# Six converted weight halves instead of five in the U pass, three raw buffers instead of five, and the split issued half a chunk sooner

## The chip, the cores and the metric

The kernel runs on one core of a Trainium2 chip. The metric is the time of one execution in microseconds, taken as the median of three runs. TensorE multiplies matrices, VectorE (DVE) and ScalarE (ACT) do elementwise work, GpSimd (POOL) issues the gathers, SyncE (SP) issues the weight loads.

## The reference, cut to what matters

One decoder layer: RMSNorm, eight differential-attention heads beside four mLSTM heads, an output projection, and then PEER, a layer of 16,384 experts of which each token takes 128. PEER dominates the time:

```python
act = jax.nn.gelu(jnp.einsum('td,tkd->tk', hb, ub), approximate=False)
return jnp.einsum('tk,tkd->td', gb * act, jnp.take(v, ib, axis=0))
```

where `ub` are the rows of the table `u` that a token's routing chose. All is float32.

## The kernel before, in words

For 352 of the 512 tokens the kernel does not gather expert rows. It multiplies the tokens by the whole table `u`, 128 chunks of 128 experts (the U pass), applies GELU, masks with a gate matrix, and multiplies by the whole table `v` (the V pass). For the other 160 tokens it gathers the chosen rows one by one: GpSimd issues an indirect DMA of 128 rows (`gather`, L834), and VectorE multiplies and adds 2048 columns of it (`run`, L861, at L846 or L859). Three row buffers `ug` rotate, so the gather after next but one waits for VectorE.

A float32 product is made of three matmuls (`mm3`, L90 to L92): weights are split into a high part `hi` and a low part `lo`, and so are the tokens. A chunk of `u` comes in two halves of 1024 columns. For each half, `load_half` (L73) loads it with an SP DMA into a buffer `raw`, ScalarE casts it to `hi` (L80), and VectorE subtracts `lo = raw - hi` (L81). A raw buffer is free again when its subtraction is done; a `hi`/`lo` buffer is free when TensorE has done its 24 matmuls of that half.

The stage that the change touches is the middle of the U pass, chunks 32 to 121 (90 of the 128), while the list `ru` is filled. There each chunk issues, in this order of the program: the split of the next chunk (`step`, L888, calls `uload(n + 1)`, L878), its own 48 matmuls, its GELU `at` on ScalarE (L902), one or two gate builds, and one or two gathered rows (`pace`, L1129). A gate build `q` is: VectorE writes one-hot masks `e` and products `eg` (`ebuild`, L1096 to L1099), ScalarE scales `ea` (L1101), TensorE multiplies them into the PSUM tile `pg` (`gbuild`, L1110, 12 matmuls), ScalarE copies `pg` to `stg` (L1118), and every eighth build one store of 2 MB from `stg` to `Gd` goes out on ScalarE's DMA queue (L1120). The 88 builds are spread over the chunks 32 to 110, so that about every tenth chunk has two. In that case TensorE multiplies both behind the same chunk, and the masks of the second are written behind the first.

TensorE, VectorE and GpSimd take their instructions in the order of the program here. ScalarE and SyncE take them in an order that the compiler's scheduler sets from its own estimates. Two PSUM tiles `pu` take the chunks in turn, two tiles `pg` the gate builds, and the masks have two buffers each.

In this stage there are five `hi`/`lo` buffers, all in the pool `wp`, and five raw buffers: three in `wp`, and two in the pool `rup`, which exists in this stage alone and takes the halves numbered 1 and 3 of every five. Buffers are 4 KB per partition each.

Of the kernel before, what the change touches and what calls it, by code (L numbers as in the profile page):

```python
# [9 lines left out]
R = mybir.dt.float32r  # L10
# [50 lines left out]
def body(tc, I, out):  # L61
    nc = tc.nc
    top = ExitStack()
    with top:
        top.enter_context(tc.manual_schedule(engines={mybir.EngineType.PE}))
        cp = top.enter_context(tc.tile_pool(name="cp", bufs=1))
        wp = top.enter_context(tc.tile_pool(name="wp", bufs=5))
        dp = top.enter_context(tc.tile_pool(name="dp", bufs=1, space=DRAM))

        def load_half(src, name, rawp=None):  # L70
            pool, n = rawp or (wp, 3)
            raw = pool.tile([128, 8, 128], F, name="raw" + name, tag="raw", bufs=n)
            nc.sync.dma_start(raw, src.rearrange("p (k c) -> p k c", k=8))  # L73
            return raw

        def split_half(src, name, raw=None, eng=nc.vector, rawp=None):
            raw = raw or load_half(src, name, rawp)
            hi = wp.tile([128, 8, 128], R, name="hi" + name, tag="whi")
            lo = wp.tile([128, 8, 128], R, name="lo" + name, tag="wlo")
            nc.scalar.copy(hi, raw)  # L80
            eng.tensor_tensor(lo, raw, hi.bitcast(F), op=OP.subtract)  # L81
            return hi, lo

        def split_tile(src, name, rawps=(None, None)):
            return [split_half(src[b], f"{name}_{b}", rawp=rawps[b]) for b in range(2)]

        def mm3(ps, w, k, xh, xl, cs):
            hi, lo = w[k // 8]
# [40 lines left out]
        def wsplit(i):  # L129
            if i < wz.shape[0] and i not in w:  # L130
                w[i] = split_tile(wz[i], f"z{i}")
# [89 lines left out]
        for k in range(KD):  # L221
            xpose(k, "m01", 0)
            if k in (2, 5):
                w[0].append(split_half(None, f"z0_{k}", raw0[k // 3], nc.gpsimd))
            if k == 6:
                sq(nc.scalar, "2", 0)
            if k == 8:
                sq(nc.vector, "2", 1)
                sq(nc.scalar, "3", 0)
            if k == 9:  # L230
                norm("2")
            if k == 10:
                sq(nc.vector, "3", 1)
                scale(nc.vector, "2", 0)
            if k == 11:
                norm("3")
                scale(nc.vector, "2", 1)
            if k == 13:
                scale(nc.vector, "3", 0)
            if k == 15:  # L240
                scale(nc.scalar, "3", 1)
            if k >= GLAG:
                gate_mm(gp[0], 0, k - GLAG)
        for k in range(KD - GLAG, KD):
            gate_mm(gp[0], 0, k)
        for k in range(KD):
            xpose(k, "23", 1)
            if k == 4:
                gate_evac(gp[0], 0)
                w[1].append(split_half(None, "z1_0", raw1))  # L250
                raw1 = load_half(wz[1, 1], "z1_1")
            if k == 12:
                w[1].append(split_half(None, "z1_1", raw1))
            if k >= GLAG:
                gate_mm(gp[1], 1, k - GLAG)
# [411 lines left out]
def rest(tc, I, out, L):  # L667
    nc = tc.nc
    wp, dp, mixT, ident, nfw = L["wp"], L["dp"], L["mixT"], L["ident"], L["nfw"]
    split_half, load_half, split_tile, mm3, rsqrt_small, big = (  # L670
        L[n] for n in ("split_half", "load_half", "split_tile", "mm3", "rsqrt_small", "big"))
# [15 lines left out]
    with tc.tile_pool(name="op", bufs=1) as op_, tc.tile_pool(name="pso", bufs=6, space=PSUM) as pso:  # L687
# [34 lines left out]
        for i, (p, pr) in enumerate(seq):  # L722
            dc, tbs = passes[p]
            if pr == 0:
# [3 lines left out]
                ps = {tb: pso.tile([128, 512], F, name="po", tag="po") for tb in tbs}  # L728
# [6 lines left out]
            hi, lo = (t.rearrange("p a b -> p (a b)") for t in ws.pop(i))  # L735
            for j in range(2):
                n = 2 * pr + j
# [6 lines left out]
            if p == 4 and pr in (2, 5):  # L744
                b = stores.pop(0)
# [44 lines left out]
    for b in range(2):  # L790
        cs = slice(1024 * b, 1024 * b + 1024)
        t = wp.tile([128, 8, 128], F, name="nfr", tag="raw", bufs=3).rearrange("p a b -> p (a b)")
        src = I["nfr"][0:1, cs]
# [82 lines left out]
    ru = []  # L876

    def uload(n):  # L878
        if n < len(sp) and n not in w:
            ps = [None, None]  # L880
            if ru:
                for b in range(2):
                    if ru[1] % 5 in (1, 3):
                        ps[b] = (ru[0], 2)
                    ru[1] += 1
            w[n] = split_tile(sp[n], f"d{n}", ps)

    def step(n, mid=None):  # L888
        uload(n + 1)
        ps = pmu.tile([128, 512], F, name="pu", tag="pu")  # L890
        nn = S if n < 16 else ND
        for k in range(KD):
            mm3(ps[:, :nn], w[n], k, h2h, h2l, slice(0, nn))
            if k == 7 and mid:
                mid()
        w.pop(n)
        return ps

    def u_chunk(c, mid=None):
        ps = step(16 + c, mid)  # L900
        at = h2p.tile([128, ND], F, name="at", tag="at", bufs=3)
        nc.scalar.activation(at, ps[:, :ND], AF.Gelu)  # L902
        nc.scalar.dma_start(Ad[c // 4, :, c % 4, :], at)

    with tc.tile_pool(name="tk", bufs=1) as tk, \
# [21 lines left out]
        def scores(h, p, qt):  # L927
            sk = tk.tile([128, 128], F, name="sk", tag="sk", bufs=2)
            nc.scalar.dma_start(sk, I["sk"][:, 2 * h + p, :])
            ps = pss.tile([128, TB, 128], F, name="pscore", tag="ps")  # L930
            for b in range(TB):
                nc.tensor.matmul(ps[:, b, :], qt[:, 128 * b:128 * b + 128], sk, start=True, stop=True)
            sc = tk.tile([128, TB, 128], F, name="scr", tag="scr", bufs=9)
            nc.scalar.copy(sc, ps)
            hd[h, p] = sc
            if p == 1:
                for b in (3, 0, 1, 2):
                    bg.append(head_tasks(h, b))
# [62 lines left out]
        def mid():  # L1001
            while pend:
                n, qt = pend.pop(0)
                scores(n // 2, n % 2, qt)
# [17 lines left out]
        for n in range(2, 16):  # L1022
            ps = step(n, mid)
            pend.append((n, qcopy(ps)))
            bgstep()
            if n % 4 == 2:
                bgstep()
# [32 lines left out]
        for src, dst in ((n1s, n1T), (n2s, n2T), (gs, None)):  # L1060
            pt = ptr.tile([128, ND], F, name="ptt", tag="ptt")
            for b in range(3):
                n = min(128, ND - 128 * b)
# [83 lines left out]
    with ExitStack() as sV:  # L1147
# [56 lines left out]
        for g in range(NG - 1):  # L1204
            n = GROUPS[g]
            free += [t0 + n + 2 * (j // 2) + 2 for j in range(n)]
            t0 += 2 * n
        for q in range(GROUPS[0], NK):
            g = max(x for x in range(NG) if g0s[x] <= q)
            m, n = q - g0s[g], GROUPS[g - 1]  # L1210
# [12 lines left out]
        for c in range(NK - UTAIL, NK):  # L1223
# [5 lines left out]
            for _ in range(-(-len(pro) // (NK - c))):  # L1229
                f, q = pro.pop(0)  # L1230
# [115 lines left out]
        for i, (g, hf, pr, c) in enumerate(vord[:last]):  # L1346
# [9 lines left out]
            if i == nlast - 8:  # L1356
                for b in range(2):
                    t = wp.tile([128, 8, 128], F, name="nlw", tag="raw", bufs=3)
                    src = I["nlw"][0:1, 1024 * b:1024 * b + 1024]
# [21 lines left out]
            else:  # L1381
                dc = hf
                if pr == 0:
                    ps = []
# [3 lines left out]
                hi, lo = vs.pop(i)  # L1388
# [6 lines left out]
                if tail:  # L1395
                    f, tb = tail.pop(0)
# [96 lines left out]
```

## Time and profile before

| what | value |
|---|---|
| median of three runs | 3291.85 us (3288.75 to 3292.93) |
| profiled execution | 3289.89 us, span 3288.1 us |
| TensorE matmul busy | 3222.9 us, 98% of the span |
| VectorE busy | 2323.8 us, 71% |
| ScalarE busy | 1315.1 us, 40% |
| GpSimd busy | 932.0 us, 28% |
| the stage with `ru` filled | about 1412 to 2205 us |

TensorE is busy nearly throughout; what a change in the preparation of weights can move is the idle time of TensorE that ends with such a piece of work. The share of VectorE is a mean over stages and is far higher in the stage of interest.

### The profile page before, as it was taken

To read this page: it belongs to the slowest core of one execution; us is meant where nothing else is said; L and a number is where in the kernel's file an instruction comes from. 1 tells how busy PE (TensorE), PEld (TensorE's weight loads), DVE (VectorE), ACT (ScalarE), POOL (GpSimd) and SP (SyncE) were. 2 spreads that over 40 slices of the span, in tenths; PEclk is the share of its full clock that TensorE was granted. 3 is DMA by queue.
4 is the path that set the end of the run, shared out by engine and by line. 5 is a ranking of instruction groups with operands and counts; after the bars stand their busy time and mean duration, and the time that the engine had idled before them with its cause. 6 is when DMAs were issued, how large, how long until landed. Compare 5 with 4: busy or idle time off the path is not lost.

```text
span 3288.1 us, 51152 instructions
## 1 busy us (share of the span) xinstructions
PE 3222.9 (98%) x20174; PEld 3038.4 (92%) x20174; DVE 2323.8 (71%) x3521; ACT 1315.1 (40%) x2219; POOL 932.0 (28%) x974
## 2 busy tenths in 40 slices
PE   8999999999999999999999999999999999999998
PEld 7889898888887899999999999999999999999997
DVE  7444444444266688888988889876787888887875
ACT  5444544444252233354544444434333333333323
POOL 2011111110007666523333344331222222222212
PEclk9999999999999999999999999999999999999999
DMA  4222122223363256679999999998998988988973
GB/s 156 71 71 78 65 72 71 65 71 109 109 211 126 90 194 220 239 285 374 388 364 389 374 367 391 388 413 292 374 336 334 373 324 332 375 320 330 362 277 139
DMA packets 230161, 815.47 MB, mean 248 GB/s; under 512 B 21696, under 2 KB 85696, under 8 KB 186528
## 3 DMA queue, kind: packets, MB, share of 16 engines
q1 hardware_dynamic: 103904, 377.65, 31.9%
q0 software_dynamic: 46080, 335.56, 26.0%
q10 hardware_dynamic: 79936, 98.98, 8.6%
q8 instruction: 158, 2.59, 0.3%
q14 instruction: 83, 0.68, 0.1%
HBM read 757.33 MB, written 54.79 MB: 247 GB/s over the span
## 4 chain that ended last, share of the span: by engine, by line
PE 64%; issue 18%; POOL 10%; DVE 4%; DMA 3%; ACT 1%; ACTq 0%; POOLq 0%; SPq 0%; DVEq 0%
PE py L1304 9%; PE py L1306 9%; PE py L1305 9%; POOL ug L838 8%; PE ps L90 6%; PE ps L92 5%; PE ps L91 5%; PE pu L90 3%; PE pu L91 3%; PE pu L92 3%; PE po L743 2%; PE po L741 2%; PE po L742 2%; DMA ug<-in_vn_dram,idxB 1%; PE pn L534 1%
## 5 line engine op out<-in xcount | busy, mean ns | idle before, releaser
L91 PE MATMUL pu<-hh,lod 128*128 128x352 f32 (+1 forms) x2272 | 756.2, 333 | 16.7 <-DVE lod L81 16.6
L90 PE MATMUL pu<-hh,hid 128*128 128x352 f32 (+1 forms) x2272 | 763.8, 336 | 2.7 <-ACT at L902 2.7
L92 PE MATMUL pu<-hl,hid 128*128 128x352 f32 (+1 forms) x2272 | 754.0, 332 | 0.0
L1305 PE MATMUL py<-ah,lov 128*128 128x352 f32 x1984 | 641.4, 323 | 5.8 <-DVE lov L81 5.8
L1304 PE MATMUL py<-ah,hiv 128*128 128x352 f32 x1984 | 644.4, 325 | 0.6 <-ACT at L902 0.6
L1306 PE MATMUL py<-al,hiv 128*128 128x352 f32 x1984 | 643.8, 325 | 0.0
L80 ACT CAST hiv<-rawv 128x1024 fp32r<-128x1024 f32 x256 | 269.0, 1051 | 549.6 <-PE py L1306 482.6
L91 PEld LDWEIGHTS pu<-hh,lod 128*128 128x128 f32 x2272 | 431.1, 190 | 27.9 <-DVE lod L81 18.5
L90 PEld LDWEIGHTS pu<-hh,hid 128*128 128x128 f32 x2272 | 431.8, 190 | 12.6 <-ACT at L902 3.0
L92 PEld LDWEIGHTS pu<-hl,hid 128*128 128x128 f32 x2272 | 431.0, 190 | 9.8
L81 DVE TENSOR_TENSOR lod<-rawd,hid 128x1024 fp32r<-128x1024 f32 x284 | 363.0, 1307 | 70.6 <-ACT hid L80 70.4
L90 PE MATMUL ps<-xh,hiz 128*128 128x256 f32 (+2 forms) x1280 | 410.3, 321 | 0.6 <-DVE qT L370 0.5
L92 PE MATMUL ps<-xl,hiz 128*128 128x256 f32 (+2 forms) x1280 | 392.5, 307 | 0.0
L91 PE MATMUL ps<-xh,loz 128*128 128x256 f32 (+2 forms) x1280 | 392.0, 306 | 0.0
L838 POOL DMA_INDIRECT ug<-in_vn_dram,idx x128 | 208.3, 1627 | 618.6 <-DVE y L859 598.2
L80 ACT CAST hid<-rawd 128x1024 fp32r<-128x1024 f32 x284 | 295.7, 1046 | 211.5 <-PE pu L92 109.2
L1305 PEld LDWEIGHTS py<-ah,lov 128*128 128x128 f32 x1984 | 372.7, 188 | 7.9 <-DVE lov L81 7.9
L1304 PEld LDWEIGHTS py<-ah,hiv 128*128 128x128 f32 x1984 | 372.8, 188 | 0.8 <-ACT at L902 0.8
L1306 PEld LDWEIGHTS py<-al,hiv 128*128 128x128 f32 x1984 | 372.0, 187 | 0.0
L838 POOL DMA_INDIRECT ug<-in_un_dram,idx x128 | 249.7, 1951 | 404.4 <-DVE ug L846 386.1
L81 DVE TENSOR_TENSOR lov<-rawv,hiv 128x1024 fp32r<-128x1024 f32 x256 | 311.8, 1229 | 64.3 <-ACT hiv L80 64.3
L846 DVE SCALAR_TENSOR_TENSOR ug<-ug,h2n 128x2048 f32<-128x2048 f32 x128 | 304.2, 2396 | 39.3 <-DMA ug<-in_un_dram,idx 39.0
(343 smaller groups left out, 4845.8 us busy)
## 6 DMA issues: line engine op xcount, KB each, us to landing
rawd<-in_u_dram SPq DMA_DIRECT2D x256, 512.0 KB, 7.5
rawv<-in_v_dram SPq DMA_DIRECT2D x256, 512.0 KB, 6.6
rawz<-in_wz_dram SPq DMA_DIRECT2D x98, 512.0 KB, 3.6
Ad<-at ACTq DMA_DIRECT2D x128, 176.0 KB, 6.2
Gd<-stg ACTq DMA_DIRECT2D x11, 2048.0 KB, 15.9
gt<-Gd ACTq DMA_DIRECT2D x32, 704.0 KB, 12.2
av<-Ad ACTq DMA_DIRECT2D x64, 352.0 KB, 6.7
rawwo<-in_wo_dram SPq DMA_DIRECT2D x40, 512.0 KB, 3.8
```

The lines of the kernel that those rows point to most:

```text
L80: nc.scalar.copy(hi, raw)
L81: eng.tensor_tensor(lo, raw, hi.bitcast(F), op=OP.subtract)
L90: nc.tensor.matmul(ps, a, xh[k][:, cs], start=(k == 0), stop=False)
L91: nc.tensor.matmul(ps, b, xh[k][:, cs], start=False, stop=False)
L92: nc.tensor.matmul(ps, a, xl[k][:, cs], start=False, stop=(k == KD - 1))
L741: nc.tensor.matmul(ps[tb], mh[n][:, sl], h, start=(n == 0), stop=False)
L742: nc.tensor.matmul(ps[tb], mh[n][:, sl], l, start=False, stop=False)
L838: nc.gpsimd.indirect_dma_start(out=t, out_offset=None, in_=I["un" if kind in "dD" else "vn"], in_offset=bass.IndirectOffsetOnAxis(ap=ix[:, ...
L846: nc.vector.scalar_tensor_tensor(t, t, 1.0, acc[kind], op0=OP.mult, op1=OP.mult, accum_out=o)
L1304: nc.tensor.matmul(po, h, ah, start=(pr + j == 0), stop=False)
L1305: nc.tensor.matmul(po, l, ah, start=False, stop=False)
L1306: nc.tensor.matmul(po, h, al, start=False, stop=(2 * pr + j == n - 1))
```

## The change

Raw buffers are three for all halves. The pool `rup` holds one more `hi` and one more `lo` in their place (the half numbered 5 of every six), so six converted halves exist at a time. And inside the stage, the split of chunk n + 2 is issued behind the first 24 matmuls of chunk n; the call at the start of a step then finds its chunk already split. In the order of VectorE, the two subtractions of a chunk now stand ahead of the mask building and the gathered rows that they stood behind.

```diff
-        def split_half(src, name, raw=None, eng=nc.vector, rawp=None):
-            raw = raw or load_half(src, name, rawp)
-            hi = wp.tile([128, 8, 128], R, name="hi" + name, tag="whi")
-            lo = wp.tile([128, 8, 128], R, name="lo" + name, tag="wlo")
+        def split_half(src, name, raw=None, eng=nc.vector, wpool=None):
+            raw = raw or load_half(src, name)
+            pool, n = wpool or (wp, 5)
+            hi = pool.tile([128, 8, 128], R, name="hi" + name, tag="whi", bufs=n)
+            lo = pool.tile([128, 8, 128], R, name="lo" + name, tag="wlo", bufs=n)
...
-                    if ru[1] % 5 in (1, 3):
-                        ps[b] = (ru[0], 2)
+                    if ru[1] % 6 == 5:
+                        ps[b] = (ru[0], 1)
...
             if k == 7 and mid:
                 mid()
+            if k == 7 and ru:
+                uload(n + 2)
```

## Rows read from the trace of the kernel before

**Rows 1.** Waits of PE, 1412 to 2205 us: total us, times, longest.
```profile
PE pu L91 <- DVE lod L81: 16.6, 6, 5.5
PE pg L1110 <- ACT ea L1101: 5.1, 3, 3.0
```

**Rows 2.** Timeline of PE: start, length, instruction, idle before and releaser.
```profile
1683.84 0.66 PE L91 MATMUL pu<-hh,lod 128*128 128x352 f32 x1 [5.52 <-DVE lod L81]
...
1841.31 0.43 PE L91 MATMUL pu<-hh,lod 128*128 128x352 f32 x1 [0.52 <-DVE lod L81]
...
1879.44 0.66 PE L91 MATMUL pu<-hh,lod 128*128 128x352 f32 x1 [4.12 <-DVE lod L81]
...
1943.57 0.43 PE L91 MATMUL pu<-hh,lod 128*128 128x352 f32 x1 [1.90 <-DVE lod L81]
```

**Rows 3.** Stretches: length, busy PE, PEld, DVE, ACT, POOL, clock, DMA, GB/s.
```profile
1500.00:1600.00 100.00, 100.00 (x708) 98.56 (x708) 88.20 (x113) 49.35 (x99) 42.71 (x20) 0.99 0.95 365
...
1683.84:1690.47 6.63, 6.63 (x25) 6.63 (x26) 6.60 (x8) 3.16 (x7) 2.35 (x2) 0.55 0.94 339
1879.44:1885.60 6.16, 6.16 (x25) 6.16 (x26) 6.13 (x9) 3.04 (x7) 1.89 (x2) 0.60 0.98 366
...
1943.57:1947.52 3.95, 3.95 (x24) 3.95 (x25) 3.92 (x6) 2.16 (x6) 0.76 (x1) 1.00 0.98 371
```

**Rows 4.** Timeline of DVE, parts of two chunks, same columns.
```profile
1875.95 2.29 DVE L846 SCALAR_TENSOR_TENSOR ug<-ug,h2n 128x2048 f32<-128x2048 f32 x1 [7.60 <-DMA ug<-in_un_dram,idx]
...
1960.89 0.42 DVE L1096 TENSOR_TENSOR e<-iota,n1T 128x512 bf16<-128x512 bf16 x1
...
1962.36 2.28 DVE L846 SCALAR_TENSOR_TENSOR ug<-ug,h2n 128x2048 f32<-128x2048 f32 x1
...
1964.57 2.35 DVE L81 TENSOR_TENSOR lod<-rawd,hid 128x1024 fp32r<-128x1024 f32 x2
```

**Rows 5.** Waits of DVE, 1815 to 2205 us: total us, times, longest.
```profile
DVE ug L846 <- DMA ug<-in_un_dram,idxB: 20.0, 10, 4.9
DVE ug L846 <- DMA ug<-in_un_dram,idx: 17.1, 6, 7.6
DVE yB L859 <- DMA ug<-in_vn_dram,idxB: 7.9, 7, 1.7
```

**Rows 6.** Timeline of DVE at three double gate builds.
```profile
1737.25 0.43 DVE L1096 TENSOR_TENSOR e<-iota,n1T 128x512 bf16<-128x512 bf16 x1 [5.88 <-PE pg L1110]
...
1890.29 0.42 DVE L1096 TENSOR_TENSOR e<-iota,n1T 128x512 bf16<-128x512 bf16 x1 [2.35 <-PE pg L1110]
...
1968.97 0.43 DVE L1096 TENSOR_TENSOR e<-iota,n1T 128x512 bf16<-128x512 bf16 x1 [0.57 <-PE pg L1110]
```

**Rows 7.** Timelines of DVE and PE at the start of the stage.
```profile
1416.23 1.22 DVE L81 TENSOR_TENSOR lod<-rawd,hid 128x1024 fp32r<-128x1024 f32 x1
1419.56 1.23 DVE L81 TENSOR_TENSOR lod<-rawd,hid 128x1024 fp32r<-128x1024 f32 x1 [2.11 <-ACT hid L80]
1420.70 0.42 DVE L1096 TENSOR_TENSOR e<-iota,n1T 128x512 bf16<-128x512 bf16 x1
...
1422.74 0.22 PE L1110 MATMUL pg<-ea,e 128*128 128x128 bf16 x1 [1.92 <-ACT ea L1101]
```

**Rows 8.** Loads of u, 1403 to 1420 us.
```profile
DMA to landing us min/median/max: 4.7/4.7/4.7
```

**Rows 9.** Loads of u, 1815 to 2205 us.
```profile
DMA to landing us min/median/max: 4.1/8.8/16.6
```

**Rows 10.** Loads of u, 1985 to 2015 us, beside a store to Gd.
```profile
DMA to landing us min/median/max: 12.0/14.3/16.6
```

**Rows 11.** Loads of u, 2116 to 2145 us, beside a store to Gd.
```profile
DMA to landing us min/median/max: 7.1/12.5/15.4
```

**Rows 12.** Loads of u, 1940 to 1985 us, beside no store.
```profile
DMA to landing us min/median/max: 5.7/7.3/8.7
```

**Rows 13.** Page, costliest groups: busy us, mean ns, idle before, releaser.
```profile
L90 PE MATMUL pu<-hh,hid 128*128 128x352 f32 (+1 forms) x2272 | 763.8, 336 | 2.7 <-ACT at L902 2.7
...
L80 ACT CAST hid<-rawd 128x1024 fp32r<-128x1024 f32 x284 | 295.7, 1046 | 211.5 <-PE pu L92 109.2 <-DMA rawd<-in_u_dram 82.1 <-issue 11.3
```

More of the change, by code (lines that the diff above doesn't have):

```diff
@@ L82, in split_half, with split_tile @@
             return hi, lo
-        def split_tile(src, name, rawps=(None, None)):
-            return [split_half(src[b], f"{name}_{b}", rawp=rawps[b]) for b in range(2)]
+        def split_tile(src, name, wps=(None, None)):
+            return [split_half(src[b], f"{name}_{b}", wpool=wps[b]) for b in range(2)]
         def mm3(ps, w, k, xh, xl, cs):
```

## The prediction

> **What bounds the kernel now.** I read the page first: TensorE is busy 98% of the span, so only its idle time, and stretches at a lower clock, can be won. Then the waits of TensorE in the stage with `ru` [rows 1]: 16.6 us in six waits for a low part `lo` from VectorE, and 5.1 us in three waits for `ea`, the last input of a gate build. The reader is to see that nothing else stops TensorE there. Four of the six waits stand in [rows 2]; the other two are later and make up the rest of the sum. A long wait costs twice. After the waits of 5.52 and 4.12 us the next half chunk took 6.63 and 6.16 us at a granted clock of 0.55 and 0.60 (a part of it at 1.2 GHz), against 3.95 us at 1.00 (2.4 GHz) after a wait of 1.90 us [rows 2, 3]: 2.7 + 2.2 = 4.9 us more. So late low parts cost TensorE 16.6 + 4.9 = 21.5 us. That is all the change can remove.
>
> Why are they late? VectorE works in program order: two subtractions (2.35 us), the masks (1.5 us, from 1960.89 to 1962.36), one or two gathered rows of 2.2 us each, and the next two subtractions [rows 4]. A gathered row that has not landed holds up all behind it. The wait of 4.12 us at 1879 comes right behind one of 7.60 us for a gather [rows 4]; from 1815 us on such waits add up to 45.0 us [rows 5]. The chunk takes TensorE 8.5 us: 60 matmuls with one gate build, and 708 were made in 100 us [rows 3]. VectorE needs 2.35 + 1.5 + 4.4 = 8.3 us when there are two rows, and so has next to nothing to make a wait good.
>
> **The change, part by part.**
>
> *The split sooner.* No instruction is added. In VectorE's order the two subtractions of chunk n + 2 change places with the masks and rows issued at the end of chunk n. Each `lo` is then ahead of up to two rows and their waits, by 1.5 + 4.4 = 5.9 us without waits, more than the largest of the six waits. I take all six as gone: -21.5 us. With six converted halves, both buffers of chunk n + 2 are free when chunk n - 1 is done, early enough for this; with five the second would wait for the middle of chunk n. The casts move too. They wait on ScalarE for a load and for a buffer, and behind them stand GELU, the copy of `pg` and `ea`, on which TensorE's next PSUM tiles and gate builds depend.
>
> *What is late next: the masks.* They now stand behind one more pair of subtractions. At a chunk with two gate builds, the second build needs masks that VectorE writes behind the split of two chunks on, and TensorE waits right there. At such places VectorE in its turn waits for the first of the two builds to free a buffer, by 5.88, 2.35 and 0.57 us in the three that follow a wait of [rows 2], [rows 6]. So both engines meet there about every ten chunks, and between two meetings VectorE has the same ten pairs to do before and after the change. A wait for `lo` that goes therefore comes back at the next meeting, less what VectorE waited there. Of 5.52 + 2.7 - 5.88 remain 2.3 us; of 0.52 + 4.12 + 2.2 - 2.35 remain 4.5; of 1.90 - 0.57 remain 1.3. Together +8.1 us. The two waits after 2060 us have no meeting behind them and go wholly.
>
> *The start.* In the first chunk of the stage, two chunks are split instead of one ahead of the masks of build 1, and TensorE already waits 1.92 us there [rows 7]. The added pair costs 2.35 us at least. With three raw buffers the load of its second half can only be issued when the subtraction of 1416.23 ends, at 1417.5; with 4.7 us to land [rows 8], a cast of 1.05 us [rows 13] and a subtraction of 1.23 us it is done at 1424.5, and the masks start there instead of at 1420.7 [rows 7]: +3.8 us. I take 3.8, since each step has a row. The wait grows to 5.7 us, about that of 1683, and the slow stretch behind it with it; I add 1.5 us, an estimate between nothing and the 2.7 us seen there. Together +5.3 us. Nothing later gives it back: the stage is 90 chunks of TensorE's pace.
>
> *Two raw buffers fewer.* The load of a chunk's second half is issued when the first subtraction of the chunk before ends, and its own turn on VectorE comes one chunk later. So 8.5 - 1.05 = 7.4 us are left for landing. Loads beside no store land in 7.3 us at the median [rows 12]: just enough. Beside a store to `Gd` they took 14.3 and 12.5 us [rows 10, 11], on average 13.4, so VectorE would wait 6.0 us. Of this the two rows that now stand behind the pair (4.4 us) are what TensorE does not need at once, which leaves 1.6 us; with one store per eight builds, five fall between 1815 and 2205 us, where VectorE has nothing to spare: +8.0 us. The bounds: nothing, if VectorE would have waited for a gather in the same time anyway; and, from the median of the whole stretch [rows 9], (8.8 - 7.4) us in each of 46 chunks (390 us at 8.5), 64 us, less the 45 us of gather waits that lie beside them [rows 5], so 19 us. I take 8.0, which is nearer to the rows for loads beside stores. SyncE issues nothing but these loads here, in order. GpSimd's gathers wait for rows to be done, so each moves back by up to one pair.
>
> On this term a rule speaks against my figure. The landing times above rise from 7.3 to 14.3 us with other traffic, under the same five buffers [rows 10, 12]. The Trainium skill, "DMA: Bandwidth & Descriptors", section "Queues, rings and completion order", says that each DMA engine goes round the queues that have work, packet by packet. By it the weight queue keeps its turn however few loads stand in it, and a load with fewer of its own kind ahead would land sooner: the term would be nothing and the sum -8.1. No run here shows loads with three buffers beside gathers.
>
> *The end of the stage.* The call for the next chunk finds its work done in step 122, and from there the order is as before. TensorE's one wait there, 2.7 us for `at` [rows 13], stays; at worst it doubles, because the sixth pair's place is now freed by matmuls.
>
> **Sum.** -21.5 + 8.1 + 5.3 + 8.0 = -0.1 us on the profiled execution of 3289.89 us, so 3289.8. The median of the runs is 1.96 us above that execution; on its scale the time is 3291.8, and I say 3292.
>
> **Rivals.**
>
> *A: the loads keep up.* The last term is nothing, as in its lower bound: -8.1 us, 3283.7. For it: VectorE idles 45.0 us on gathers, in which loads can land [rows 5]. Against it: the first load of a pair has 7.4 us and needs 7.3 even without a store [rows 12]. The rule of the Trainium skill cited above comes out at this case.
>
> *B: VectorE waits for raw halves.* Place: the second subtraction of each pair, once loads land in more than 7.4 us on average. Behind it wait the masks and rows, and on ScalarE, behind the cast, `ea` and `at`. Price 19 instead of 8.0: +10.9 us, 3302.8. For it: the median landing is 8.8 us already [rows 9]. Against: fewer loads in flight also leave the DMA engines freer.
>
> *C: the change does not do what it says*, because ScalarE's order, which the scheduler sets, puts the casts where they were; then `lo` is as late as now, 3292, in the same class as the forecast.
>
> **How the numbers follow.** A measurement of this kernel tells about 0.2% (6.6 us) from no change. Forecast 0.40, with C 0.04 beside it; A 0.28; B 0.28. Faster is A, slower is B, the same is the rest. The likeliest case's own range is 3286 to 3298. The range reaches 4.7 us below A (a start that costs the bare pair, 2.35 instead of 5.3, and a smaller remainder at the meetings) and 2.2 us above B (the doubled wait of 2.7 at the end, about): 3279 to 3305.
>
> **What would show it.** TensorE's waits for `lod` in the stage fall from 16.6 to below 4 us, and those for `ea` rise from 5.1 to over 12, one of some 5.7 us near 1424 and others at double builds. VectorE's waits for `hid` lie between 10 and 40 us. If `lod` waits stay above 10 us, the order was not what mattered. If `ea` waits stay near 5 us, the meetings are wrong and the time is near A or below. If `hid` waits on VectorE pass 40 us, B is right.

## The result, and the profile after

The changed kernel takes 3335.14 us (3331.96 to 3338.81, 4 runs) where the kernel before took 3290.3 on the same chip: ratio 1.0139 [1.0126, 1.0152], slower by 44.8 us. The forecast was 3292, the range 3279 to 3305, and the chance of slower 0.28.

Where the time went is read from the GELU of chunk 31 to that of chunk 127, that is from chunk 32 to the end of the U pass, at the same work (the profile holds 7 matmul records fewer after). Columns: stretch, its length, and busy time and instructions of PE, PEld, DVE, ACT, POOL, then TensorE's clock, DMA share and GB/s. Before:

```profile
1411.54:2255.49 843.95, 819.37 (x5673) 805.96 (x5671) 712.30 (x870) 389.53 (x745) 302.93 (x160) 0.98 0.96 374
```

After:

```profile
1413.50:2302.70 889.20, 830.65 (x5666) 816.44 (x5664) 712.84 (x870) 390.59 (x744) 307.79 (x160) 0.96 0.92 355
```

45.2 us of loss are here, of the 46.6 between the two profiled executions (3336.5 and 3289.89). VectorE's and ScalarE's work is the same to 1.1 us. TensorE's busy time grew by 11.3 us for the same matmuls, at a clock of 0.96 instead of 0.98; the other 34.0 us are waits. These are the waits of TensorE (total, times, longest) that answer to [rows 1], 1412 to 2243 us:

```profile
PE pg L1113 <- DVE eg L1102: 31.4, 7, 7.6
PE pg L1113 <- ACT ea L1104: 13.6, 4, 4.7
PE pu L91 <- ACT at L905: 2.0, 1, 2.0
```

Not one wait for a low part is left, of 16.6 us; the gate builds wait 45.0 us instead of 5.1. So the masks are late now, eleven times, nine of these at the second of two builds behind one chunk. What makes VectorE late stands in its own waits of the same stretch:

```profile
DVE lod L82 <- ACT hid L81: 84.0, 35, 7.3
DVE ug L847 <- DMA ug<-in_un_dram,idx: 36.2, 15, 6.4
DVE ug L847 <- DMA ug<-in_un_dram,idxB: 14.8, 4, 6.9
...
DVE yB L860 <- DMA ug<-in_vn_dram,idxB: 4.4, 2, 3.8
```

Before, 1412 to 2205 us, it had waited for other things:

```profile
DVE ug L846 <- DMA ug<-in_un_dram,idx: 39.0, 17, 7.6
DVE e L1096 <- PE pg L1110: 24.3, 13, 5.9
DVE ug L846 <- DMA ug<-in_un_dram,idxB: 20.0, 10, 4.9
DVE lod L81 <- ACT hid L80: 8.7, 4, 3.4
DVE yB L859 <- DMA ug<-in_vn_dram,idxB: 7.9, 7, 1.7
```

Waits for casts rose by 75.3 us. In the balance, 24.3 of them came out of the waits for TensorE at the meetings, which are gone, and 12 out of the gather waits (68 to 55). The rest, 39 us, is time. Of the 84.0 us, 72.5 stand before the second subtraction of a chunk, 31 times of 35. The casts in turn wait for loads; ScalarE's waits after, over the same stretch, and the row of the page that answers to [rows 13]:

```profile
ACT hid L81 <- DMA rawd<-in_u_dram: 306.6, 120, 8.1
```

```profile
L81 ACT CAST hid<-rawd 128x1024 fp32r<-128x1024 f32 x284 | 296.9, 1047 | 429.6 <-DMA rawd<-in_u_dram 325.1
```

Before it was 82.1 on that row. And yet the loads did not land later. 1815 to 2205 us after, to be held against [rows 9] (the trace has a landing time for 64 of the 84 loads here, and for 47 of 89 before):

```profile
DMA to landing us min/median/max: 3.8/7.8/15.6
```

One place shows the whole chain. VectorE after, at a chunk with two builds:

```profile
1903.28 2.29 DVE L847 SCALAR_TENSOR_TENSOR ug<-ug,h2n 128x2048 f32<-128x2048 f32 x1 [6.38 <-DMA ug<-in_un_dram,idx]
...
1905.50 2.36 DVE L82 TENSOR_TENSOR lod<-rawd,hid 128x1024 fp32r<-128x1024 f32 x2
...
1909.24 2.28 DVE L847 SCALAR_TENSOR_TENSOR ug<-ug,h2n 128x2048 f32<-128x2048 f32 x1
...
1911.45 1.22 DVE L82 TENSOR_TENSOR lod<-rawd,hid 128x1024 fp32r<-128x1024 f32 x1
1914.37 1.23 DVE L82 TENSOR_TENSOR lod<-rawd,hid 128x1024 fp32r<-128x1024 f32 x1 [1.71 <-ACT hid L81]
1915.52 0.42 DVE L1099 TENSOR_TENSOR e<-iota,n1T 128x512 bf16<-128x512 bf16 x1
...
1916.31 0.76 DVE L1102 TENSOR_TENSOR eg<-e,gp 128x512 bf16<-128x512 bf16 x2
```

ScalarE and TensorE there:

```profile
1913.30 1.04 ACT L81 CAST hid<-rawd 128x1024 fp32r<-128x1024 f32 x1 [2.86 <-DMA rawd<-in_u_dram]
```

```profile
1916.76 0.26 PE L1113 MATMUL pg<-ea,e 128*128 128x128 bf16 x1 [6.06 <-DVE eg L1102]
```

It begins with a gather: VectorE waits 6.38 us for a row, and the subtraction behind it frees its raw buffer only at 1906.72. The load into that buffer goes out at 1906.75 and its cast starts at 1913.30, 6.6 us on, so the load itself is not slow; it was issued late. The subtraction waits 1.71 us for this cast, and the masks for the second build stand behind it. The gather wait and the wait for the cast come one after the other, and not side by side.

The start, answering to [rows 7], VectorE and TensorE:

```profile
1418.81 3.49 DVE L82 TENSOR_TENSOR lod<-rawd,hid 128x1024 fp32r<-128x1024 f32 x3
1427.41 1.23 DVE L82 TENSOR_TENSOR lod<-rawd,hid 128x1024 fp32r<-128x1024 f32 x1 [5.12 <-ACT hid L81]
1428.56 0.42 DVE L1099 TENSOR_TENSOR e<-iota,n1T 128x512 bf16<-128x512 bf16 x1
```

```profile
1429.80 0.27 PE L1113 MATMUL pg<-ea,e 128*128 128x128 bf16 x1 [7.61 <-DVE eg L1102]
```

And the end of the stage, ScalarE with its queue, VectorE, TensorE:

```profile
2257.19 1.05 ACT L81 CAST hid<-rawd 128x1024 fp32r<-128x1024 f32 x1 [7.65 <-DMA rawd<-in_u_dram]
...
2260.99 1.04 ACT L81 CAST hid<-rawd 128x1024 fp32r<-128x1024 f32 x1 [2.75 <-DMA rawd<-in_u_dram]
2261.37 0.38 ACTq L1161 DMA_DIRECT2D gt<-Gd  x1
```

```profile
2268.29 0.53 DVE L1168 TENSOR_TENSOR tm<-av,gt 128x352 f32<-128x352 f32 x1 [14.20 <-DMA av<-Ad]
2268.73 2.36 DVE L82 TENSOR_TENSOR lod<-rawd,hid 128x1024 fp32r<-128x1024 f32 x2
```

```profile
2262.45 0.43 PE L91 MATMUL pu<-hh,hid 128*128 128x352 f32 x1 [2.44 <-ACT at L905]
2270.01 0.66 PE L92 MATMUL pu<-hh,lod 128*128 128x352 f32 x1 [7.13 <-DVE lod L82]
```

The V pass's first loads go out 17 us behind the start of chunk 122, where before they went out 11 us ahead of it. VectorE stands before `tm`, with the split of chunk 124 behind.

By the first matmuls of the chunks, after against before, 6.0 us are lost in chunk 32, 32.6 from there to the start of chunk 122, and 7.3 from there to the end of the pass.

### The profile page after: what moved, and what is told of

The parts are those of the page before. It is cut to its first block, busy times and chain, and to the rows that moved or that the text cites. A ratio compares the mean times of both kernels' runs of the same rounds, so it can differ in the third digit from the quotient of the medians.

```text
span 3334.7 us, 51142 instructions
## 1 busy us (share of the span) xinstructions
PE 3237.2 (97%) x20170; PEld 3051.3 (92%) x20174; DVE 2324.4 (70%) x3521; ACT 1317.0 (39%) x2219; POOL 934.5 (28%) x974
## 4 chain that ended last, share of the span: by engine, by line
PE 63%; issue 19%; POOL 10%; DVE 3%; DMA 3%; ACT 1%; POOLq 0%; ACTq 0%; SPq 0%; DVEq 0%
PE py L1307 9%; PE py L1309 9%; PE py L1308 9%; POOL ug L839 8%; PE ps L91 5%; PE ps L93 5%; PE ps L92 5%; PE pu L92 3%; PE pu L91 3%; PE pu L93 3%; PE po L744 2%; PE po L742 2%; PE po L743 2%; DMA ug<-in_vn_dram,idxB 1%; PE pn L535 1%
## 5 line engine op out<-in xcount | busy, mean ns | idle before, releaser
L91 PEld LDWEIGHTS pu<-hh,hid 128*128 128x128 f32 x2272 | 434.7, 191 | 16.8 <-ACT at L905 7.2
L92 PEld LDWEIGHTS pu<-hh,lod 128*128 128x128 f32 x2272 | 433.8, 191 | 16.9 <-DVE lod L82 7.4
## 6 DMA issues: line engine op xcount, KB each, us to landing
gt<-Gd ACTq DMA_DIRECT2D x32, 704.0 KB, 11.3
```

The source lines that it names most:

```text
L91: nc.tensor.matmul(ps, a, xh[k][:, cs], start=(k == 0), stop=False)
L92: nc.tensor.matmul(ps, b, xh[k][:, cs], start=False, stop=False)
```

## The experiments

Theory 1 in the first four: three raw buffers make VectorE wait for casts. Theory 2: the masks are late because they stand behind one more pair of subtractions, whatever the buffers. Each time is given with that of the kernel before on the same chip.

### The change taken apart

**Order alone**, on the kernel before:

```diff
             if k == 7 and mid:
                 mid()
+            if k == 7 and ru:
+                uload(n + 2)
```

> Five raw buffers and five converted halves as before, only the split half a chunk sooner. Theory 1, three raw buffers make VectorE wait for casts (84 us in the changed kernel's stage, 8.7 before) and the masks behind them come late: with five raw buffers these waits fall below 30 us, TensorE's waits for the gate builds from 45 us to below 20, and the time is 3291 to 3302. Theory 2, the masks are late because they stand behind one more pair of subtractions, whatever the buffers: TensorE still waits 40 us or more at the double builds, 3320 to 3340.

3306.07 against 3287.08: 1.0055 [1.0038, 1.0072], 19.0 us slower, between the two. The `lod` waits are 0.3 us, the gate builds wait 34.9 (1400 to 2290 us). The profile points to a third reason. With five pairs the second half of chunk n + 2 needs a pair that TensorE frees in the middle of chunk n; ScalarE waits there (47.6 us before) and VectorE behind it (21.0 before):

```profile
ACT hid L80 <- PE pu L92: 116.8, 64, 5.0
```

```profile
DVE lod L81 <- ACT hid L80: 62.8, 37, 12.0
```

**Buffers alone**: the changed kernel without those two lines, so six pairs, three raw buffers, the split at its old place.

> Six converted halves and three raw buffers, with the split where it was before. Theory 1: VectorE waits 60 to 100 us for casts in the stage as in the changed kernel, TensorE now waits for the low parts instead of the builds, 3305 to 3330. Theory 2: no more waits than before, 3285 to 3295.

3333.85 against 3287.08: 1.0137 [1.012, 1.0154], 46.8 us. It is above the range of theory 1: the buffers cost all, not half. Nor does TensorE wait for low parts in the main: 9.0 us, against 21.0 for `ea` and 16.9 for `at` (1400 to 2290 us).

**Three raw buffers and nothing else**, on the kernel before:

```diff
-                    if ru[1] % 5 in (1, 3):
+                    if False:
                         ps[b] = (ru[0], 2)
```

> Three raw buffers, five converted halves, the split where it was before: the two extra raw buffers are taken away and nothing is given for them. Theory 1: within 6 us of the kernel with six halves and three raw buffers, since the sixth half has nothing to do when loads are late, 3305 to 3330. Theory 2: as before, 3285 to 3295.

3334.16 against 3287.08: 1.0144 [1.0127, 1.0161], 47.1 us, as much as buffers alone and as the whole change. Theory 2 falls. VectorE waits for casts as in the changed kernel, with the old order; TensorE waits for the gate builds and, unlike there, for `at` (1400 to 2290 us):

```profile
DVE lod L81 <- ACT hid L80: 106.7, 41, 9.0
```

```profile
PE pg L1110 <- ACT ea L1101: 34.7, 12, 9.8
PE pu L90 <- ACT at L902: 23.3, 9, 16.0
```

**Masks first**, on the kernel before; the split stands sooner than before but behind the masks:

```diff
                 gcopy(ng - 1)
+            uload(16 + c + 2)
             pace(c)
```

> Before's five and five buffers; the split of chunk n + 2 stands behind the masks of chunk n's builds and ahead of its gathered rows. Both theories: the waits for low parts go, as in the changed kernel. Theory 1: the builds are not late either, so TensorE's waits in the stage fall from 21.7 us to below 8, 3270 to 3283. Theory 2: the same. If it comes out above 3290, VectorE has a third cause to be late.

3289.44 against 3287.08: 1.0009 [0.9999, 1.0018], a miss. The 16.6 us of `lod` waits are gone and 21.9 of gate builds stand in their place:

```profile
PE pg L1110 <- DVE eg L1099: 14.4, 5, 4.6
PE pg L1110 <- ACT ea L1101: 7.5, 3, 4.5
```

What the one piece gained, the other lost. VectorE also waits 57.1 us for casts here instead of 21.0 (1400 to 2290 us), so the five pairs may have a part in it, as in order alone; this run does not tell the two apart.

**The change without its price.** Six pairs beside five raw buffers do not fit beside the 16 KB buffer of the stores; with stores of 16 tokens (`TG = 16`) they do.

> The change without its price: six converted halves and five raw buffers, the split half a chunk sooner. To make room, the stores to Gd take 16 tokens instead of 32 each, so there are 22 of 1 MB instead of 11 of 2 MB, and the V pass reads runs of 256 bytes instead of 512; the kernel before with such stores is to be run as its control. Theory 1, the missing raw buffers are the whole loss: below its control, by about 21.5 - 8.1 = 13 us less a start and an end of up to 10, so 3280 to 3292 us if the small stores cost nothing. Theory 2, the sooner split costs by itself, as it did with five converted halves (19 us): 3300 to 3312 us.

> The kernel before with stores to Gd of 16 tokens (22 of 1 MB instead of 11 of 2 MB): the control for the kernel with six converted halves and five raw buffers, which took 3291.1 us. Theory 1, without the loss of raw buffers the change gains 3 to 13 us: then this control is at 3294 to 3304. Theory 2, the change is worth nothing by itself: 3287 to 3293.

The control took 3284.63 against 3289.65, 0.9987 [0.9976, 0.9998]; six pairs with five raw buffers 3291.11 against 3290.05, 1.0008 [0.9999, 1.0018]. By the two ratios the early split with its sixth pair is some 0.2% slower than its control, although no buffer was taken for it; theory 1's gain is not there, and the control came out below the ranges of both theories. In the profiles, by the chunks' first matmuls, it lost 4.8 us against the control in chunks 32 and 33, won 6.9 back by chunk 117, and ends the U pass 2.4 us better than it entered the stage. What it takes longer in these profiles, 4.1 us, lies behind the stage, at the start of the V pass, where its granted clock is 0.97 instead of 1.00 and it makes 536 matmuls in 100 us instead of 562. Single executions of the kernel before lie between 3278.66 and 3297.94 us, so differences of a few us between two profiles say little. Its `lod` waits fell from 6.5 us to none within the stage, and its gate builds' rose from 11.1 to 16.5. VectorE's waits for casts are 8.2 us there (1405 to 2200 us): with the sixth pair the third reason of order alone is gone.

**The end.** The same kernel, early split no further than chunk 122:

```diff
-            if k == 7 and ru:
+            if k == 7 and ru and n + 2 <= 16 + NK - UTAIL:
```

> Six converted halves, five raw buffers, small stores, as before, but the sooner split stops with chunk 122, so that chunk 123 is split in its old place, at the start of the step of chunk 122. In the kernel without this, VectorE stood 14.2 us before tm for the first load of av, with the subtractions for chunk 124 behind it, and 12 us were lost between chunks 122 and 124. If ScalarE's order, in which the loads for the V pass follow the sooner casts, is the cause, 9 to 12 us come back: 3279 to 3284 us. If the space for these loads is, the wait stays: 3288 to 3293.

3293.42 against 3289.65: 1.002 [1.0011, 1.003]. Nothing came back. The 12 us had been read from the times of the GELUs, which ScalarE's order moves; by the chunks' first matmuls, against the kernel before, the kernel without the limit loses 3.0 us from chunk 117 to the end of the pass, and the one with it 8.6. Yet this does not clear ScalarE's order: the limit did not bring the V pass's loads forward. They go out 19 us behind the start of chunk 122, behind both casts of chunk 124, and without the limit 8 us behind it, also behind those casts. The same holds in every kernel with a sixth pair, buffers alone among them (15 us behind, the split at its old place), while the kernel before has them 11 us ahead and the one with nothing in `rup` (three raw buffers) 76 us ahead. So the late loads come with the sixth pair and not with the early split. Whether by the pair's space or by ScalarE's order was not tested.

### What makes three buffers too few

**Four raw buffers**, on the kernel before (one in `rup`, for one half in four):

> The kernel before with four raw buffers for u in the stage (three in the fixed pool, one in the stage's own), five converted halves and the split where it was. Theory 1, a buffer's round trip: with three raw buffers one goes round in 14.1 us on average (landing 8.75, wait for the cast 0.6, cast 1.05, wait for the subtraction 2.5, subtraction 1.2), so a half comes every 4.7 us where TensorE takes 4.2; four buffers have 16.9 us for the same trip and more than enough: 3287 to 3300 us. Theory 2, there is no such threshold, each buffer less costs its share because the DMA engines are 97% busy before and every idle microsecond of theirs is lost: half the loss of three buffers, 3305 to 3318 us.

3297.67 against 3290.05: 1.0024 [1.0014, 1.0035]. From five to four 7.6 us, from four to three 39.5: a bend between four and three, as theory 1 says.

**Half the gathered rows**, as a base and with three raw buffers:

```diff
...
+        m = msz[j] = 64 if ru and kind in "dD" else 128
-        nc.gpsimd.indirect_dma_start(out=t, out_offset=None, in_=I["un" if kind in "dD" else "vn"],
-                                     in_offset=bass.IndirectOffsetOnAxis(ap=ix[:, k:k + 1], axis=0))
+        nc.gpsimd.indirect_dma_start(out=t[0:m], out_offset=None, in_=I["un" if kind in "dD" else "vn"],
+                                     in_offset=bass.IndirectOffsetOnAxis(ap=ix[0:m, k:k + 1], axis=0))
...
```

> The kernel before with half the gathered data in the stage: the gathers of rows of un take 64 of 128 tokens, and VectorE multiplies those 64 partitions alone, in the same time; the other 64 tokens get no contribution from them. 142 gathers bring 0.5 MB less each, 71 of 300 MB. It is the base for the next kernel. If the gathers' landing is what makes VectorE late before (its waits for gathered rows are 67 us), TensorE's waits of 24 us and the slow clock behind them go: 3255 to 3275 us. If VectorE's own work is what makes it late, 3280 to 3290 us.

> The kernel with three raw buffers, five converted halves and the split at the old place, with half the gathered data as in the kernel before with half rows. Theory 1, round trip: the loads land in about 5 us when a quarter of the traffic is gone, the trip takes about 10.4 us of the 12.7 that three buffers have, and the loss of 47 us goes: within 8 us of the kernel before with half rows. Theory 2, three buffers tie the loads to the subtractions in VectorE's order, whatever the landing: 20 us or more above it.

The base took 3299.18 against 3290.05, 1.0027 [1.0014, 1.0039]; with three buffers it was 3344.39 (3330.68 to 3366.39), 1.0188 [1.015, 1.0226]. Both missed, because the relief did not come: see the last section. By its letter the second result speaks for theory 2; but the time from a load's issue to its cast did not fall (9.0 us against 9.1 with full rows), so theory 1 would not have the loss go either.

**Half loads**, as a base and with three raw buffers:

```diff
+            if small[0]:
+                nc.sync.dma_start(raw[:, 0:4], src.rearrange("p (k c) -> p k c", k=8)[:, 0:4])
+                return bcast_mid(raw[:, 0:4].rearrange("p b c -> p (b c)"), 2)
...
```

> The kernel before, in which each load of the stage brings only the first 512 of a half's 1024 columns (0.25 MB instead of 0.5), and the cast and the subtraction read these columns twice, in the same time and into the same buffers; the other columns of u in the stage are replaced by these. It is the base for the next kernel. Gathers and loads share the DMA engines with 46 of 300 MB less: 3270 to 3288 us.

> The kernel with three raw buffers, five converted halves and the split at the old place, with the half loads of the kernel just named. It shortens the landing by itself and leaves every buffer, queue and order as they are. Theory 1, round trip: landing falls from 8.75 us to 4 to 6, the trip from 14.1 to 9.5 to 11.4 us, under the 12.7 that three buffers have at TensorE's pace, and the loss of 47 us goes: within 10 us of the kernel before with half loads. Theory 2, three buffers tie each load to VectorE's order and the landing matters little: 20 us or more above it.

3273.81 (0.9964 [0.9951, 0.9976]) and 3292.27 (1.0007 [0.9997, 1.0017]), against 3289.65. Three buffers cost 18.5 us here instead of 47.1: between the theories, and nearer to the mark of theory 2. Theory 1 had counted on a landing of 4 to 6 us, and half the bytes shortened issue to cast only from 9.1 to 7.6 us.

**No gathers**, VectorE's rows kept, for the kernel before, three raw buffers, and the change:

```diff
+        if ru and kind in "dD":
+            rows[j] = kept[j] = kept[j - 3]
+            return
...
```

> The kernel before without the DMA of 142 gathers of rows of un in the stage: VectorE works the same number of rows, each in the same time, on buffers that were filled before the stage (with a maximum in place of the product, so that values stay finite); their part of the result is replaced by that. It is the base for the two kernels below. The waits for gathered rows (67 us) go and loads meet hardly any other traffic; TensorE's 24.5 us of waits and some 10 us of slow clock go for the most part: 3255 to 3270 us.

> The kernel with three raw buffers, five converted halves and the split at the old place, without those gathers. Theory 1, round trip: a load alone on the DMA engines lands in 4 to 5 us (4.7 at the start of the stage), the trip takes some 9 of the 12.7 us that three buffers have at TensorE's pace, and the loss of 47 us, of which half loads took away 28, goes wholly: within 6 us of the base without gathers. Theory 2, the tie to VectorE's order (rows of 2.2 us before each subtraction) is a cost of its own: 15 us or more above the base.

> The changed kernel without those gathers. Theory 1: as in the kernel before without gathers, but for a start of some 2 us and an end of up to 9: 0 to 11 us above the base, and VectorE's waits for casts fall from 87 to under 20 us. Theory 2: 20 us or more above it.

3246.28, 3245.83 and 3260.73, against 3286.44: 0.9869 [0.9844, 0.9894], 0.9868 [0.9843, 0.9893], 0.9917 [0.9891, 0.9943]. The base came out 9 us below its range. Without the gathers, two raw buffers fewer cost nothing, in the same order and on the same engines. 1420 to 2200 us, first the kernel before without gathers, then with three buffers:

```profile
1420.00:2200.00 780.00, 778.77 (x5501) 768.03 (x5501) 696.42 (x851) 380.18 (x723) 24.61 (x17) 1.00 0.58 205
```

```profile
1420.00:2200.00 780.00, 777.73 (x5496) 766.57 (x5494) 696.31 (x851) 385.84 (x723) 27.65 (x17) 1.00 0.59 206
```

TensorE is busy 99.8% and 99.7% of the time, with VectorE doing all its rows. The change is 14.5 us above its base, a little more than theory 1 gave it: 7.5 us in chunks 32 and 33, 2.5 until chunk 123, 4.3 until the end of the pass. VectorE's waits for casts fell to 36.4 us and not under 20. Most of the loss is the start and the end; the one long wait:

```profile
PE pg L1118 <- DVE eg L1107: 7.5, 1, 7.5
```

**Seven raw buffers**, five pairs, stores of 16 tokens (four raw buffers in `rup`):

> The kernel before with stores of 16 tokens, and in the room that this leaves two more raw buffers for u, seven in all; five converted halves and the split at the old place. From five raw buffers to four cost 7.6 us, from four to three 36 more. Theory 1, a threshold: five are already above it, and seven give at most 4 us on the 3284.6 us of the kernel with small stores alone: 3280 to 3287. Theory 2, every buffer more is reserve against late loads: 3270 to 3279.

3281.98 against 3286.44: 0.9977 [0.9962, 0.9992]. It beats the kernel before and the changed one, by little more than the small stores do alone: no gain of seven buffers over five can be told. That there is none is not shown: in the profiles its V pass is 5.7 us longer than the control's (1039.4 against 1033.7), which may hide a gain in the stage.

### The sum that orders them

A raw buffer goes round: issue, landing, cast, subtraction, and the next load is issued 0.03 us later. Worked out from each load, cast and subtraction of chunks 34 to 117 (168 halves), issue to cast took 9.3 us on average after, cast and subtraction 1.05 + 1.22. At TensorE's pace a half takes 4.22 us (the kernel before without gathers), so n buffers have 4.22 n us. What is left is the time by which VectorE may come late to a half that lies ready.

| kernel | raw buffers | issue to cast | time left | loss to its base |
|---|---|---|---|---|
| before | 5 | 12.4 | 6.5 | - |
| before, no gathers, three | 3 | 5.0 | 5.4 | 0 |
| four | 4 | 10.6 | 4.0 | 7.6 |
| after, no gathers | 3 | 7.3 | 3.1 | 14.5, of it 2.5 between start and end |
| three, half loads | 3 | 7.6 | 2.8 | 18.5 |
| three, half rows | 3 | 9.0 | 1.4 | 45.2 |
| three | 3 | 9.1 | 1.3 | 47.1 |
| after | 3 | 9.3 | 1.1 | 44.8 |

VectorE's rows are 2.2 us each [rows 4] and its gather waits up to 7 us; with 1.1 us left, each of them can delay the next load, as at 1903. Two raw buffers were the reserve against them. Issue to cast holds any wait of ScalarE too, so the column is an upper bound of the landing, and it is measured in each kernel: the table orders the losses, it does not forecast them. The average also hides that the two halves of a chunk differ. VectorE does their subtractions back to back, so the second half's buffer comes free late and is wanted early; after the change a second half took 8.0 us from issue to cast and a first half 10.5, and most of VectorE's waits for casts stand at second halves.

The gathers do two things at once, they fill the DMA engines and they hold VectorE; the half loads, which leave VectorE's work and order as they are, gave back 28.6 of 47.1 us. The rest was not separated.

## Why the prediction was wrong

**The low parts (-21.5).** Right: 16.6 us went to nothing in the stage, in every kernel with the earlier split. With three raw buffers and the split at its old place they went too (0.2 us), while TensorE waited for `ea` and `at` instead, so the changed kernel alone would not show it; masks first and six pairs with five buffers do. What does not follow is that it is a gain.

**The meetings (+8.1).** Right in kind: both engines do the same ten pairs between two double builds, and what one wait gives the other takes. The amount was too small even with enough buffers: with masks first 16.6 us went and 16.8 came, and with six pairs and five raw buffers the start took 4.8 of the 6.9 us that the stage gave.

**The start (+5.3).** Near, 6.0, and the load of the second half was the last piece, as worked out. The two parts missed to opposite sides: that load took 6.2 us to land and not 4.7, and TensorE's wait grew by 5.7 us instead of 3.8; the slower stretch behind it left some 0.3 us of the 1.5. That the sum came so close is in part luck.

**Two raw buffers fewer (+8.0, at most 19).** This is the step that failed, and three buffers alone show it: 47.1 us. It gave the load of a second half 7.4 us to land, held that against a median of 7.3 beside no store, called it just enough, and so counted a loss only beside five stores. The place and the budget were right, the reading of the median was not: where half of the loads take longer than the budget, half of them are late. After the change (chunks 34 to 117) 64 of 84 second halves went from issue to cast outside the 16 us behind the issue of a store. They took 7.2 us on average, 33 of them more than 7.4, and 44.2 us of VectorE's waits stand before them, against 23.6 before the 20 beside stores. Over both halves the trip of a buffer was 13.9 us, 9.3 from issue to cast and 2.3 of waiting for VectorE among it, for the 12.7 that three buffers have.

And the upper bound took off 45 us of gather waits as lying beside the waits for casts. They do not: a gather wait holds up the subtraction, and the next load goes out later for it. Of 75.3 us more for casts only 12 came out of the gathers' waits, 24.3 out of the meetings'. It also counted from 1815 us on; by chunk 80 (1840 us before) 23 us were already lost.

Beside that step stood a rule of the Trainium skill, "DMA: Bandwidth & Descriptors", section "Queues, rings and completion order", that each DMA engine goes round the queues that have work, packet by packet. The trace agrees in the direction that the prediction drew from it: the median landing, of the loads that have one, fell from 8.8 to 7.8 us with fewer loads in flight. The traffic of that stretch fell as well, from 387 to 365 GB/s, so this is no proof of the rule. One microsecond was no match for two buffers.

**The end (0, at most 2.7).** Too small: waits of 2.44 and 7.13 us stand where 2.7 stood, 6.9 us more, and chunks 122 to 127 took 7.3 us longer. The prediction had the sixth pair's place in its bound, but not the V pass's first loads, which go out late in every kernel with that pair.

**The rivals.** B named the mechanism and the place, and its mark (over 40 us of waits for casts) was passed at 84.0; its price, +10.9, had the same bad bound as the forecast's. A was wrong by the same step. C fell with the `lod` waits.

## What to carry to other kernels

Price a buffer by its round trip: average time from issue to the last use, in the order that the consumer really works, against buffers times the pace. Where what is left is less than the longest thing that the consumer does in between, each of these things can delay a load, and a loss no longer stays small. A median landing equal to the time that there is means that half of the loads are late. Before moving work on an engine that is late at two kinds of deadlines, ask whether the other kind has slack; here each order paid what the other had saved.

## What the runs showed of the hardware

Halving the gathered rows from 128 partitions to 64 took the traffic from 379 to 276 GB/s and freed nothing: the DMA engines' share stayed. The kernel before with half rows, 1420 to 2200 us:

```profile
1420.00:2200.00 780.00, 747.80 (x5222) 733.41 (x5221) 669.06 (x824) 359.70 (x700) 272.78 (x153) 0.98 0.98 276
```

VectorE's waits for gathered rows were 80 us instead of 68 (1412 to 2205 us), and the kernel was 9 us slower than with whole rows. The Trainium skill, "SBUF — State Buffer", section "Door 1: The DMA port swizzle (why `[64,N]` ≈ `[32,N]`)", says that the DMA rate depends on how many of 16 ports the partitions reach; by its table the lower 64 partitions reach one of the two ports of each cluster. The lower rate here fits, but no run here tells it from other causes, such as the address pattern of the shorter gather.

The share is therefore no measure of how much the DMA engines still could move: 0.98 stood beside 276 GB/s, and 0.97 beside 379 in the kernel before.

Of the 45.2 us lost, 11.3 were matmuls at a lower granted clock, 0.96 over the stretch instead of 0.98. Where TensorE's waits went, in the kernel before and with three buffers, both without gathers, it was 1.00.
